# Gated inputs of a two-layer decoder trunk: token scales behind fewer or more gates, low parts on GpSimd, two halves in one PSUM bank

## The chip, the cores and the metric

The program runs on one core of one Trainium2 chip. The metric is device time in microseconds for one execution, the median over the runs of a comparison. All tensors are float32; the kernel splits every operand of a product into a high part, which TensorE takes in its reduced float32 form (`fp32r`), and a low part, the remainder, and adds three products (high by high, high by low, low by high). The engines are TensorE (PE; its weight loads are PEld), VectorE (DVE), ScalarE (ACT), GpSimd (POOL) and SyncE (SP), each with a queue of its own that runs in order.

## The reference

Two layers over 512 tokens of width 1024. The part that the change touches closes each layer:

```python
for i in range(DEPTH):
    h = h + 0.5 * swiglu(rmsnorm(h, nw[0]), ffn_w_in[i, 0], ffn_w_out[i, 0])
    hn = rmsnorm(h, nw[1])
    h = h + (retention if i == 0 else forgetting_attention)(hn, ...)
    h = h + 0.5 * swiglu(rmsnorm(h, nw[2]), ffn_w_in[i, 1], ffn_w_out[i, 1])
    gate = jax.nn.sigmoid(rmsnorm(h, nw[3]) @ ple_w_gate[i])      # 1024 x 1024
    h = h + gate * (p[i] @ ple_w_proj[i])                         # p: 512 x 256
return rmsnorm(h, final_norm_w)
```

`rmsnorm` scales each token by the root of its mean square, and `retention` and `forgetting_attention` are the two token mixers.

## The kernel before

Activations lie transposed: `h` is eight blocks of 128 channels by 512 tokens in SBUF (one tile, `hall`). A product with a 1024-wide weight gives one such block, 24 matmuls of 512 columns (8 blocks of the contraction, 3 products each, line 296 to 298 in `mm3`).

Work on TensorE runs in the order in which the program is written. The other engines' orders come from a scheduler that places each instruction by priority when its buffers can be had. Four FFNs are numbered 0 to 3; FFN 1 ends layer 0's chain before the first gated input, FFN 2 opens layer 1, FFN 3 stands before the second gated input.

Weights come through `Weights`: SyncE loads a chunk of 128 x 1024 into one of four raw tiles (`wraw`), ScalarE casts the high part (line 78), and the engine that `W.low` names subtracts to get the low part (line 79). Chunks go into three `w8` tiles, in the order of a plan, two ahead of the one in use. Where `W.low` is `nc.vector`, the low part is VectorE's, where it is `nc.gpsimd`, GpSimd's. A chunk is called hereafter p0, p1 (projection, four output blocks each) and g0 to g7 (gates); the plan is p0, g0 to g4, p1, g5 to g7, and then FFN 2's chunks.

A normalization is not applied ahead of a product: the product runs on `h` times the gain, and its result is multiplied by the token scales. `n.columns()` sums the squares over channels on TensorE (8 small matmuls, line 310) and computes the scales by a short chain on VectorE and ScalarE (lines 446 to 455); `n.rows()` spreads them over the partitions by 4 transposes (line 443) and a copy (line 437) to a tile `rows`.

A gated input (`ple`) has for each of eight output blocks m: a gate product (`gates`, 24 matmuls), a projected input (`added`, 6 matmuls), and `rest`: VectorE multiplies the gate's bank by `rows` (line 1093), ScalarE takes the sigmoid (1094), VectorE multiplies by the projected bank (1097) and adds to `h` (1098). In layer 0 all 512 tokens go at once (`parts == 1`), and behind each `rest` stands `nxt.block(m)`, which makes the eighth part of FFN 2's input forms (lines 353 to 400: sums and differences of token halves on VectorE, high parts on ScalarE, low parts on VectorE) and adds a square to the norm's sum. FFN 2's first two output blocks (`plain`, line 507) need all eight, the last ones at the end of the first half's products. In layer 1 the tokens go in two halves of 256 (`parts == 2`); `W.emit` first issues the chunks up to p0, g0, g1 with the current `W.low`, and the other seven get tiles that stay until the second half: g2 and g3 in eight tiles of a pool `unit_b`, five in a pool of their own. Behind it come the final norm and the output.

PSUM has eight banks of 128 x 512; the pool hands out whole banks, and a bank is free once its last reader is done. The order of work before: added(0..2), gates 0 and 1 interleaved, gate 2, columns, gate 3, rows, added(3), rests 0 to 3, and then gate m, added(m), rest m for m from 4.

Of the kernel before, what the change touches and what calls it, by code (L numbers as in the profile page):

```python
# [54 lines left out]
class Weights:  # L55
# [103 lines left out]
    def take(self, src):  # L159
        assert self.plan[self.used] is src  # L160
        self.emit(self.used + 1 + LOOKAHEAD)
        self.used += 1
        return self.ready[self.used - 1]
# [9 lines left out]
def trunk(ctx, tc, a):  # L173
    nc = tc.nc
# [15 lines left out]
    W = Weights(nc, wraw, wpool)  # L190

    def unit(pool):
        return pool.tile([P, S], F32R, name="unit_" + {id(ua): "a", id(ub): "b", id(uc): "c", id(ud): "d"}[id(pool)])
# [17 lines left out]
    ple_g = [[a["ple_gate"][l, m] for m in range(KB)] for l in range(2)]  # L211
# [60 lines left out]
    def bank():  # L272
        return psum.tile([P, S], F32, name="bank")

    def temp(dtype=F32):
        return tmp.tile([P, S], dtype, name="tmp")
# [18 lines left out]
    def mm3(out, wh, wl, xh, xl, first, last):  # L295
        nc.tensor.matmul(out, wh, xh, start=first, stop=False)  # L296
        nc.tensor.matmul(out, wh, xl, start=False, stop=False)  # L297
        nc.tensor.matmul(out, wl, xh, start=False, stop=last)  # L298
# [158 lines left out]
    def proj(srcs, n, out=None, cols=slice(0, S), take=W.take):  # L457

        ws = [take(s) for s in srcs]
        os = out or [bank() for _ in ws]  # L460
        for k in range(KB):
            ks = slice(k * P, (k + 1) * P)
            for o, (wh, wl) in zip(os, ws):
                mm3(o, wh[:, ks], wl[:, ks], n.hi[k][:, cols], n.lo[k][:, cols], k == 0, k == KB - 1)
        return os
# [595 lines left out]
    def ple(l, n, nxt, phi, plo, parts=1):  # L1061

        w = S // parts
        with ExitStack() as pools:
            if parts > 1:
                W.emit(W.limit)
                W.pool = pools.enter_context(tc.tile_pool(name="wkept", bufs=KEPT - 2, reuse_waits="tile"))
                W.spare = [lambda: unit(ub)] * 8
                W.limit = len(W.plan)
            ws = {}  # L1070

            def weights(src):
                if id(src) not in ws:
                    ws[id(src)] = W.take(src)
                return ws[id(src)]

            for part in range(parts):
                ts_ = slice(part * w, (part + 1) * w)

                def gates(ms):  # L1080
                    return proj([ple_g[l][m] for m in ms], n, [bank()[:, :w] for _ in ms], ts_, weights)

                def added(m):
                    wp = weights(ple_p[l][m // 4])
                    o = bank()[:, :w]
                    for k in range(2):
                        ks = slice(((m % 4) * 2 + k) * P, ((m % 4) * 2 + k + 1) * P)
                        mm3(o, wp[0][:, ks], wp[1][:, ks], phi[k][:, ts_], plo[k][:, ts_], k == 0, k == 1)
                    return o

                def rest(m, g, o):
                    t1, t2, hm = temp()[:, :w], temp()[:, :w], h[m][:, ts_]
                    nc.vector.tensor_tensor(out=t1, in0=g, in1=n.r[:, ts_], op=ALU.mult)
                    nc.scalar.activation(t1, t1, AF.Sigmoid)
                    if parts > 1 and m == KB - 1:
                        nc.scalar.activation(warm, t1[:, 0:1], AF.Sqrt)
                    nc.vector.tensor_tensor(out=t2, in0=o, in1=t1, op=ALU.mult)
                    nc.vector.tensor_tensor(out=hm, in0=hm, in1=t2, op=ALU.add)
                    if parts == 1:
                        nxt.block(m)  # L1100
                    else:
                        nxt.new = m == 0
                        nxt.square(m, ts_, keep=m == KB - 1)
                        nc.gpsimd.tensor_scalar(out=hm, in0=hm, scalar1=fw[:, m : m + 1], scalar2=None, op0=ALU.mult)

                m = 0
                if part == 0:
                    os = [added(m) for m in range(3)]
                    gs = gates((0, 1))
                    W.low = nc.gpsimd if nxt.forms is None else nc.vector  # L1110
                    gs += gates((2,))
                    n.columns()
                    gs += gates((3,))
                    n.rows()
                    os.append(added(3))
                    for m in range(4):
                        rest(m, gs[m], os[m])
                    m = 4
                while m < KB:
                    g = gates((m,))[0]  # L1120
                    rest(m, g, added(m))
                    if part > 0 and m == 2:
                        diag = final_scale(nxt, slice(ts_.start - w, ts_.start))
                    if part > 0 and m == 4:
                        final(diag, slice(ts_.start - w, ts_.start))
                    m += 1
            W.low = nc.vector
            if parts > 1:
                final(final_scale(nxt, ts_), ts_)

    def final_scale(n, ts_):

        w = ts_.stop - ts_.start
        nb = w // P
        totals = [bank() for _ in range(nb)]
        for i, t in enumerate((n.acc[:, ts_], n.kept)):
            for j in range(nb):
                nc.tensor.matmul(
                    totals[j][:, 0:2], t[:, j * P : (j + 1) * P], ones[:, 0:2], start=i == 0, stop=i == 1
                )  # L1140
        r, v, t = (stat.tile([P, nb], F32, name=x) for x in ("last", "cv2", "ct2"))
        for j in range(nb):
            mean_eps(v[:, j : j + 1], totals[j][:, 0:1])
        rsqrt(r, v, t)
        diag = temp()[:, :w]
        nc.vector.tensor_tensor(
            out=diag.rearrange("p (j t) -> p j t", j=nb), in0=ident.unsqueeze(1).to_broadcast([P, nb, P]),
            in1=r.unsqueeze(2).to_broadcast([P, nb, P]), op=ALU.mult,
        )
        return diag  # L1150

    def final(diag, ts_):
        w = ts_.stop - ts_.start
        rows, copy = bank()[:, :w], temp()[:, :w]
        nc.tensor.matmul(rows, ones, diag, start=True, stop=True)
        nc.scalar.copy(copy, rows)
        ov = a["outT"].rearrange("(b p) t -> p b t", p=P)
        for b in range(KB):
            hb = h[b][:, ts_]
            if b < 2:  # L1160
                nc.gpsimd.tensor_tensor(out=hb, in0=hb, in1=copy, op=ALU.mult)
            else:
                nc.vector.tensor_tensor(out=hb, in0=hb, in1=rows, op=ALU.mult)
        for b0, b1, eng in ((2, 4, nc.sync), (4, 6, nc.scalar), (0, 2, nc.scalar), (6, 8, nc.sync)):
            eng.dma_start(out=ov[:, b0:b1, ts_], in_=hall[:, b0:b1, ts_])
# [24 lines left out]
    def ffn_ple(i, l, n, mid, nxt, stack, apool, parts):  # L1190
        phi, plo = [], []

        def load():
            pv = a["pT"][l].rearrange("(b p) t -> b p t", p=P)
            for b in range(2):
                t1 = temp()
                nc.sync.dma_start(out=t1, in_=pv[b])
                phi.append(unit(uc))
                plo.append(unit(uc))
                split(t1, phi[b], plo[b])  # L1200

        ffn(i, n, mid, stack, apool, load)
        stack = open_ffn(i + 1) if i < 3 else None
        ple(l, mid, nxt, phi, plo, parts)
        return stack
# [101 lines left out]
```

## Time and profile before

| | |
|---|---|
| median of 3 runs | 2255.05 us (2253.7 to 2256.75) |
| profiled execution, its own time | 2254.57 us |
| its span in the trace | 2252.8 us |
| mean granted TensorE clock | 0.983 |
| PE busy | 2158.8 us (96%) |
| DVE busy | 1467.5 us (65%) |
| ACT busy | 1211.5 us (54%) |
| POOL busy | 436.7 us (19%) |

Times in the trace are from the start of the span. The first gated input runs on TensorE from about 1137.6 to 1196.6 us, FFN 2's first output block from there to 1226.7; the second gated input begins at about 2173 us and reaches to the end. A row of a timeline gives the start, the duration, engine, line, operation, tiles, shape and count, and in brackets the idle time of the engine just before and what ended it. Where a wait hangs on several events, the row names the one that came last.

### The profile page before, as it was taken

Reading aid. Unit: us, or ns where it says so; the run is one execution under the profiler, and the core shown is the slowest. Engines: PE = TensorE matmul, PEld = TensorE weight load, DVE = VectorE, ACT = ScalarE, POOL = GpSimd, SP = SyncE. Lnnn points to the kernel's source line nnn. Section 1 sums busy time; section 2 is a strip of 40 time slices with the busy share of each in tenths; the row PEclk is TensorE's granted clock in tenths of the full one; section 3 lists DMA queues with packets and bytes.
Section 4 is the critical chain, followed back from the end, with each engine's and each line's share of the span. In section 5 each row is a group of like instructions: output and inputs, shape, how many; then the busy total and the mean of one; then the engine's idle time right before and its main releaser. Section 6 shows DMA issues by size and latency. Waiting matters only on the chain.

```text
span 2252.8 us, 34423 instructions
## 1 busy us (share of the span) xinstructions
PE 2158.8 (96%) x13501; PEld 1940.0 (86%) x13501; DVE 1467.5 (65%) x2661; ACT 1211.5 (54%) x2050; POOL 436.7 (19%) x326
## 2 busy tenths in 40 slices
PE   7999999999999899999997999999899999999998
PEld 7899997888888698988976999898778798999987
DVE  8686766353442876766758677775764686877764
ACT  7465553333233664554545656464786775554553
POOL 0010003444444010110110001013333200110144
PEclk9999999999999999999998999999999999999999
DMA  5465462222222354654522456463222234655531
GB/s 179 104 164 150 137 159 94 88 90 84 86 84 75 108 144 128 154 137 122 133 97 85 113 150 164 129 166 94 88 81 76 75 105 116 166 146 143 150 103 38
DMA packets 84882, 264.98 MB, mean 118 GB/s; under 512 B 9312, under 2 KB 12896, under 8 KB 84720
## 3 DMA queue, kind: packets, MB, share of 16 engines
q1 hardware_dynamic: 63328, 209.78, 28.2%
q0 software_dynamic: 20160, 51.91, 13.8%
q8 instruction: 106, 1.74, 0.3%
q10 hardware_dynamic: 1232, 1.09, 0.2%
q14 instruction: 56, 0.46, 0.1%
HBM read 260.62 MB, written 2.13 MB: 117 GB/s over the span
## 4 chain that ended last, share of the span: by engine, by line
PE 78%; DVE 8%; ACT 6%; issue 3%; DMA 3%; POOL 1%; SPq 0%; DVEq 0%; ACTq 0%; POOLq 0%
PE bank L476 30%; PE bank L298 13%; PE bank L296 13%; PE bank L297 13%; DMA wraw<-in_ffn_w_in 3%; PE bank L507 2%; PE bank L679 2%; PE bank L680 2%; PE bank L681 2%; DVE w L79 1%; DVE sums L140 1%; ACT p L982 1%; ACT w L78 1%; POOL w L79 1%; ACT p L984 1%
## 5 line engine op out<-in xcount | busy, mean ns | idle before, releaser
L78 ACT CAST w<-wraw 128x1024 fp32r<-128x1024 f32 (+1 forms) x245 | 248.6, 1022 | 456.0 <-PE bank L298 276.0
L298 PE MATMUL bank<-unit_a,w 128*128 128x512 f32 x736 | 287.4, 391 | 4.8 <-DVE w L79 3.1
L296 PE MATMUL bank<-unit_a,w 128*128 128x512 f32 x736 | 288.8, 392 | 2.1 <-ACT w L78 2.1
L78 ACT CAST s<-sums 128x512 fp32r<-128x512 f32 x328 | 197.7, 617 | 166.2 <-DVE sums L140 113.8
L297 PE MATMUL bank<-unit_a,w 128*128 128x512 f32 x736 | 286.9, 390 | 0.2 <-DVE unit_a L288 0.2
L79 DVE TENSOR_TENSOR s<-sums,s 128x512 fp32r<-128x512 f32 x328 | 220.4, 685 | 90.6 <-ACT s L78 90.1
L298 PE MATMUL bank<-unit_d,w 128*128 128x512 f32 (+1 forms) x712 | 270.2, 380 | 6.4 <-DVE w L79 6.4
L296 PE MATMUL bank<-unit_d,w 128*128 128x512 f32 (+1 forms) x712 | 271.2, 381 | 2.8 <-ACT w L78 1.8
L79 POOL TENSOR_TENSOR w<-wraw,w 128x1024 fp32r<-128x1024 f32 x90 | 217.0, 2414 | 287.2 <-ACT w L78 275.3
L297 PE MATMUL bank<-unit_d,w 128*128 128x512 f32 (+1 forms) x712 | 270.2, 379 | 1.8 <-DVE unit_d L288 1.8
L79 DVE TENSOR_TENSOR w<-wraw,w 128x1024 fp32r<-128x1024 f32 (+1 forms) x155 | 179.5, 1164 | 40.2 <-ACT w L78 40.0
L118 POOL DMA_DIRECT2D a<-in_ffn_w_in x82 | 71.8, 876 | 684.9 <-ACT a L117 531.8
L476 PE MATMUL bank<-unit_b,s 128*128 128x256 f32 x904 | 191.3, 278 | 0.0
L476 PE MATMUL bank<-unit_a,s 128*128 128x256 f32 x1314 | 188.4, 281 | 2.0 <-ACT unit_a L360 1.0
L476 PE MATMUL bank<-unit_d,s 128*128 128x256 f32 x1140 | 179.0, 277 | 0.0
L476 PEld LDWEIGHTS bank<-unit_a,s 128*128 128x128 f32 x1314 | 169.8, 192 | 3.0 <-ACT unit_a L360 1.2
L568 DVE SCALAR_TENSOR_TENSOR tmp<-bank,rows 128x512 f32<-128x512 f32 x96 | 66.0, 689 | 162.8 <-PE bank L298 161.5
L298 PEld LDWEIGHTS bank<-unit_a,w 128*128 128x128 f32 x736 | 138.2, 188 | 36.1 <-DVE w L79 5.3
L296 PEld LDWEIGHTS bank<-unit_a,w 128*128 128x128 f32 x736 | 138.3, 188 | 32.8 <-ACT w L78 4.5
L298 PEld LDWEIGHTS bank<-unit_d,w 128*128 128x128 f32 x712 | 136.0, 191 | 32.6 <-DVE w L79 8.3
L297 PEld LDWEIGHTS bank<-unit_a,w 128*128 128x128 f32 x736 | 138.3, 188 | 28.3 <-DVE unit_a L288 0.5
L296 PEld LDWEIGHTS bank<-unit_d,w 128*128 128x128 f32 x712 | 136.3, 191 | 30.2 <-ACT w L78 3.4
(266 smaller groups left out, 4754.4 us busy)
## 6 DMA issues: line engine op xcount, KB each, us to landing
wraw<-in_ffn_w_in SPq DMA_DIRECT2D x174, 512.0 KB, 4.2
wraw<-in_ffn_w_out SPq DMA_DIRECT2D x64, 512.0 KB, 5.1
w<-in_ffn_w_in POOLq DMA_DIRECT2D x58, 512.0 KB, 5.5
a<-in_ffn_w_in POOLq DMA_DIRECT2D x82, 256.0 KB, 6.2
wraw<-in_ffn_w_out SPq DMA_DIRECT2D x32, 384.0 KB, 3.8
wraw<-in_ret_qk SPq DMA_DIRECT2D x16, 512.0 KB, 3.5
wraw<-in_ret_v SPq DMA_DIRECT2D x16, 512.0 KB, 3.6
wraw<-in_ret_g SPq DMA_DIRECT2D x16, 512.0 KB, 3.5
```

The lines of the kernel that those rows point to most:

```text
L78: self.nc.scalar.copy(hi, raw)
L79: self.low.tensor_tensor(out=lo, in0=raw, in1=hi.bitcast(F32), op=ALU.subtract)
L118: self.nc.gpsimd.dma_start(out=lo, in_=src, accum_op=ALU.add)
L296: nc.tensor.matmul(out, wh, xh, start=first, stop=False)
L297: nc.tensor.matmul(out, wh, xl, start=False, stop=False)
L298: nc.tensor.matmul(out, wl, xh, start=False, stop=last)
L476: add = lambda w, x, start, stop: nc.tensor.matmul(out, w, x, start=start, stop=stop, skip_group_check=True)
L507: nc.tensor.matmul(o[:, HALVES[t]], x[:, ks], y, start=k == t == q == 0, stop=k == KB - 1 and q == 2, skip_group_check=True,)
L568: nc.vector.scalar_tensor_tensor(out=t1, in0=o, scalar=-0.5, in1=n.r, op0=ALU.mult, op1=ALU.mult)
L679: nc.tensor.matmul(os[t], xh, wh[:, js], start=k == 0, stop=False)
L680: nc.tensor.matmul(os[t], xh, wl[:, js], start=False, stop=False)
L681: nc.tensor.matmul(os[t], xl, wh[:, js], start=False, stop=k == KB - 1)
```

## The change

Only `ple` is changed.

In layer 0 `W.low` is GpSimd from the start of the gated input to its end (it was VectorE throughout), so g1 to g7, p1 and FFN 2's first two chunks get their low parts there. The order becomes added(0..2), gate 0, columns, gate 1, rows, added(3), rest 0, gate 2, rest 1, gate 3, rests 2 and 3, and on from m = 4 as before: the scales stand behind one gate (columns) and two (rows), where they stood behind three and four.

In layer 1 the two products of an output block share one bank, the projected input in the left 256 columns, the gate in the right. The order becomes added(0..3), gates 0 to 3 interleaved, columns, gate 4, rows, rests 0 to 3, added(4), rest 4, and on from m = 5; the second half of the tokens keeps its order. `W.low` is GpSimd from before the first product (it was set after gates 0 and 1), which moves the low parts of g2 and g3 as well.

```diff
+                both = {}
+                def half(m, i):
+                    if parts == 1:
+                        return bank()
+                    if m not in both:
+                        both[m] = bank()
+                    return both[m][:, i * w : (i + 1) * w]
+
                 def gates(ms):
-                    return proj([ple_g[l][m] for m in ms], n, [bank()[:, :w] for _ in ms], ts_, weights)
+                    return proj([ple_g[l][m] for m in ms], n, [half(m, 1) for m in ms], ts_, weights)
                 def added(m):
                     wp = weights(ple_p[l][m // 4])
-                    o = bank()[:, :w]
+                    o = half(m, 0)
...
                 if part == 0:
-                    os = [added(m) for m in range(3)]
-                    gs = gates((0, 1))
-                    W.low = nc.gpsimd if nxt.forms is None else nc.vector
-                    gs += gates((2,))
+                    W.low = nc.gpsimd
+                    os = [added(m) for m in range(2 + parts)]
+                    gs = gates((0,)) if parts == 1 else gates((0, 1, 2, 3))
                     n.columns()
-                    gs += gates((3,))
+                    m = len(gs)
+                    gs += gates((m,))
                     n.rows()
-                    os.append(added(3))
-                    for m in range(4):
+                    if parts == 1:
+                        os += [added(3)]
+                        rest(0, gs[0], os[0])
+                        gs += gates((2,))
+                        rest(1, gs[1], os[1])
+                        gs += gates((3,))
+                    for m in range(2 if parts == 1 else 0, 4):
                         rest(m, gs[m], os[m])
                     m = 4
+                    if parts > 1:
+                        rest(4, gs[4], added(4))
+                        m = 5
                 while m < KB:
                     g = gates((m,))[0]
                     rest(m, g, added(m))
```

After the change the lines of `rest` are ten further down: 1093, 1094, 1097 and 1098 become 1103, 1104, 1107 and 1108.

How instructions move is seen at three places. First VectorE in the first gated input, from the last step of the token scales (L452) to the first form (L372); the numbered tiles `w` are weight chunks, here p1 and g5 in the numbering of before:

```order
 L452 SCALAR_TENSOR_TENSOR cols<-ct,cols 128x4
-L79 TENSOR_TENSOR w_11130<-wraw,w_11130 128x1024
-L1093 TENSOR_TENSOR tmp<-bank,rows 128x512
-L1097 TENSOR_TENSOR tmp<-bank,tmp 128x512
-L1098 TENSOR_TENSOR hall<-hall,tmp 128x512
-L79 TENSOR_TENSOR w_11263<-wraw,w_11263 128x1024
+L1103 TENSOR_TENSOR tmp<-bank,rows 128x512
+L1107 TENSOR_TENSOR tmp<-bank,tmp 128x512
+L1108 TENSOR_TENSOR hall<-hall,tmp 128x512
 L372 TENSOR_TENSOR tmp<-tmp 128x256
```

The low parts of weights are gone from VectorE's queue; the rest's three instructions and the forms keep their order. One weight low (FFN 2's third chunk, `w_11521`) stays on VectorE, between the last L1103 and the last L1107.

Then ScalarE at the end of the first gated input, after the change; `w_11444` and `w_11521` are FFN 2's second and third chunks, `a` and `s` its first pair:

```order
L78 CAST w_11444<-wraw 128x1024
L365 ACTIVATE tmp<-hall,small 128x512
L290 ACTIVATE unit_a<-hall,small 128x256
L368 CAST unit_d<-tmp 128x256
L360 CAST unit_d<-tmp 128x256
L412 ACTIVATE tmp<-hall 128x512
L78 CAST w_11521<-wraw 128x1024
L1104 ACTIVATE tmp<-tmp 128x512
L116 CAST a_11660<-wraw 128x512
L117 ACTIVATE a_11660<-wraw 128x512
L78 CAST s_11656<-sums 128x512
L380 ACTIVATE tmp<-hall,small 128x512
```

Before, the casts of those two chunks stood next to each other ahead of block 4's forms, where they now stand on either side of block 6's; L380 at the end is the start of block 7's forms.

Last GpSimd before the second gated input, where `acc` is the norm's sum of squares. Before:

```order
L79 TENSOR_TENSOR w_21807<-wraw,w_21807 128x1024
L79 TENSOR_TENSOR w_21855<-wraw,w_21855 128x1024
L416 TENSOR_TENSOR acc<-acc,tmp 128x512
L79 TENSOR_TENSOR w_21938<-wraw,w_21938 128x1024
L79 TENSOR_TENSOR w_21967<-wraw,w_21967 128x1024
L79 TENSOR_TENSOR w_21990<-wraw,w_21990 128x1024
```

Now, from the fourth addition on:

```order
+L416 TENSOR_TENSOR acc<-acc,tmp 128x512 x4
+L79 TENSOR_TENSOR unit_b<-wraw,unit_b 128x512
+L416 TENSOR_TENSOR acc<-acc,tmp 128x512
+L79 TENSOR_TENSOR unit_b<-wraw,unit_b 128x512 x2
+L416 TENSOR_TENSOR acc<-acc,tmp 128x512
+L79 TENSOR_TENSOR unit_b<-wraw,unit_b 128x512
+L79 TENSOR_TENSOR w_21763<-wraw,w_21763 128x1024
+L79 TENSOR_TENSOR w_21768<-wraw,w_21768 128x1024
+L416 TENSOR_TENSOR acc<-acc,tmp 128x512
```

Four halves of g2 and g3 (`unit_b`) have come from VectorE in among the additions, ahead of g4 and p1. In the same listing of waits, L1103 of an output block in the second gated input now waits for TensorE's projected input as well, and L1107 behind it waits for ScalarE alone.

## The prediction

> **What bounds the kernel now.** I read the page first, then the chain of waits, the TensorE timeline with its waits, the table of stretches, and the VectorE, ScalarE and GpSimd timelines at the same places.
>
> ```profile
> span 2252.8 us, 34423 instructions
> PE 78%; DVE 8%; ACT 6%; issue 3%; DMA 3%; POOL 1%; SPq 0%; DVEq 0%; ACTq 0%; POOLq 0%
> ```
>
> TensorE carries the chain, so only stretches where it waits can give time. The TensorE timeline (start, us, engine, line, tiles, and in brackets the idle time before and its releaser) has these in and behind the two gated inputs:
>
> ```profile
> 1141.68 0.39 PE L296 MATMUL bank<-unit_a,w 128*128 128x512 f32 x1
> ...
> 1153.23 0.50 PE L296 MATMUL bank<-unit_a,w 128*128 128x512 f32 x1 [0.50 <-ACT w L78]
> 1154.48 0.50 PE L298 MATMUL bank<-unit_a,w 128*128 128x512 f32 x1 [0.52 <-DVE w L79]
> 1167.82 0.50 PE L296 MATMUL bank<-unit_c,w 128*128 128x512 f32 x1 [1.23 <-ACT rows L437]
> 1196.63 0.75 PE L507 MATMUL bank<-unit_b,w 128*128 128x256 f32 x5
> ...
> 1217.87 2.16 PE L507 MATMUL bank<-unit_c,w 128*128 128x256 f32 x6 [3.32 <-ACT unit_c L360]
> 1226.68 0.95 PE L310 MATMUL bank<-ones_r,tmp 128*128 128x2 f32 x8
> ...
> 2179.78 0.58 PE L298 MATMUL bank<-unit_d,w 128*128 128x256 f32 x1 [3.69 <-DVE w L79]
> 2195.17 0.38 PE L296 MATMUL bank<-unit_c,w 128*128 128x256 f32 x1 [0.68 <-ACT rows L437]
> ```
>
> The table of stretches gives us, busy time (and count) by engine, granted clock, DMA share:
>
> ```profile
> 1137.60:1196.60 59.00, 56.75 (x253) 46.17 (x252) 33.05 (x56) 28.31 (x42) 2.10 (x2) 1.00 0.27 89
> 1196.60:1226.70 30.10, 16.56 (x98) 14.74 (x97) 27.75 (x51) 19.02 (x36) 1.76 (x2) 0.72 0.32 87
> 2179.80:2184.80 5.00, 5.00 (x23) 5.00 (x24) 2.81 (x2) 4.14 (x6) 4.79 (x3) 0.50 0.29 105
> ```
>
> Gated input 0 keeps TensorE busy 56.75 of 59 us. The big hole is behind it: FFN 2's first block, 96 matmuls of 256 columns, takes 30.1 us with VectorE busy for 27.75. The last forms it needs (unit_c, from block 7) come at 1217.8, and the rest after them takes 8.8 (1217.87 to 1226.68). So gated input 0 is worth what it does to VectorE's chain of rests and forms. The first and last of those rests are dated by their last addition to h (VectorE timeline), and the forms by ScalarE's high part:
>
> ```profile
> 1170.57 0.69 DVE L1098 TENSOR_TENSOR hall<-hall,tmp 128x512 f32<-128x512 f32 x1
> 1177.96 0.69 DVE L1098 TENSOR_TENSOR hall<-hall,tmp 128x512 f32<-128x512 f32 x1
> 1185.05 0.69 DVE L1098 TENSOR_TENSOR hall<-hall,tmp 128x512 f32<-128x512 f32 x1
> 1189.46 0.69 DVE L1098 TENSOR_TENSOR hall<-hall,tmp 128x512 f32<-128x512 f32 x1
> 1194.96 0.48 DVE L291 SCALAR_TENSOR_TENSOR unit_a<-hall,small,unit_a 128x256 fp32r<-128x256 f32 x1
> 1196.35 0.68 DVE L1098 TENSOR_TENSOR hall<-hall,tmp 128x512 f32<-128x512 f32 x1
> 1202.43 0.68 DVE L1098 TENSOR_TENSOR hall<-hall,tmp 128x512 f32<-128x512 f32 x1
> 1209.91 0.68 DVE L1098 TENSOR_TENSOR hall<-hall,tmp 128x512 f32<-128x512 f32 x1
> 1214.95 0.68 DVE L1098 TENSOR_TENSOR hall<-hall,tmp 128x512 f32<-128x512 f32 x1
> ...
> 1217.20 0.62 ACT L360 CAST unit_c<-tmp 128x512 fp32r<-128x512 f32 x1
> ```
>
> **Gated input 0: an earlier start.** The three waits before the first rest (0.50, 0.52, 1.23) go, as g2's buffer comes free after one gate and os3 no longer needs the spread's bank. They give nothing by themselves, because FFN 2 then waits for VectorE. The start of the rests counts. A matmul costs 0.23 (56.75 less some 1.5 for columns and spread, over 240), a gate of 24 about 5.5, a projected block of 6 about 1.4. From 1141.7, gate 0 ends at 1147.2, columns at 1148.0, gate 1 at 1153.5, the spread at 1154.1, added(3) at 1155.5. ScalarE then runs, in its new order, a cast, rows, a cast, the table load, the sigmoid, at these durations:
>
> ```profile
> 1166.24 1.04 ACT L78 CAST w<-wraw 128x1024 fp32r<-128x1024 f32 x1 [3.87 <-issue]
> 1167.19 0.58 ACT L437 COPY rows<-bank 128x512 f32<-128x512 f32 x1
> 1167.79 1.28 ACT L1094 ACT_TABLE_LOAD   x1
> 1169.18 0.63 ACT L1094 ACTIVATE tmp<-tmp 128x512 f32<-128x512 f32 x1
> ```
>
> The second cast waits for added(3), so the sigmoid ends at 1158.6, L1107 at 1159.2, and rest 0 at about 1160.1 (it was 1171.3): **11.2 us earlier**. g1's low ahead of the last acc addition costs that sum about 2 us, under gate 0.
>
> **Gated input 0: the lows on GpSimd.** Ten lows move. The groups of L79 (min/median/max ns) price one at 2.39 on GpSimd against 1.22 on VectorE:
>
> ```profile
> L79 POOL TENSOR_TENSOR w<-wraw,w x90: 2345/2394/2875, 370.7 to 2186.7; 128x1024 fp32r<-128x1024 f32 x90
> L79 DVE TENSOR_TENSOR w<-wraw,w x155: 946/1217/1227, 17.9 to 2178.5; 128x1024 fp32r<-128x1024 f32 x123, 128x768 fp32r<-128x768 f32 x32
> ```
>
> They are not off VectorE's path. In gated input 1, where both engines already share the work, the two timelines show:
>
> ```profile
> 2172.72 2.50 POOL L79 TENSOR_TENSOR w<-wraw,w 128x1024 fp32r<-128x1024 f32 x1 [0.34 <-ACT w L78]
> 2175.49 2.55 POOL L79 TENSOR_TENSOR w<-wraw,w 128x1024 fp32r<-128x1024 f32 x1 [0.27 <-ACT w L78]
> ...
> 2173.20 2.57 DVE L79 TENSOR_TENSOR unit_b<-wraw,unit_b 128x512 fp32r<-128x512 f32 x1 [0.27 <-ACT unit_b L78]
> 2175.69 0.68 DVE L568 SCALAR_TENSOR_TENSOR tmp<-bank,rows 128x512 f32<-128x512 f32 x1
> 2176.40 2.19 DVE L571 TENSOR_TENSOR hall<-hall,tmp 128x512 f32<-128x512 f32 x1
> 2178.51 1.21 DVE L79 TENSOR_TENSOR w<-wraw,w 128x1024 fp32r<-128x1024 f32 x1
> ```
>
> A 0.69 us VectorE instruction whose two inputs lie in SBUF ends 0.55 after the GpSimd low that ran when it came (2175.77 against 2175.22, 2178.59 against 2178.04); L568, with a PSUM input, is not held. [...]
>
> L1103 and L1107 read PSUM; L1108 and all form work are exposed. The step from rest 2 to 3 has no low in it: 4.4 us. From 3 to 4 it is 6.9, less two L291 (0.4 each) and a 0.25 rest of a low: 5.85. Seven steps without lows: 4 x 4.4 + 3 x 5.85 = 35.2. Before they took 44.4 (1170.57 to 1214.95), 9.2 for lows, casts waiting for TensorE, L291 and FFN 2's sums. After the change, six lows (p1, g5, g6, g7, FFN 2's first two) fall between rest 0 and rest 7. Stepping both queues by these durations, each low starts as its cast ends, sigmoid and L1107 cover 0.2 to 1.3 of it, and the rest is held: 1.2, 1.8, 2.2, 1.4, 2.2, 2.4, in all 11.2. Four L291 1.6, the one low left on VectorE 1.2, one sum 0.6 (the others come behind rest 7), casts 0.8: 50.6. So rest 7 ends at 1210.7, and L380, one cast and the high part (0.72 + 0.5 + 0.6) put unit_c at 1212.5 instead of 1217.8. TensorE then needs the same 8.8, since it has waited as long: **-5.3 us**. Bounds: nothing held gives unit_c near 1201.3 and, with the clock up, 53 matmuls of 0.12 behind it, so 1207.7 instead of 1226.7: -19. Six times the longest low (2.88) is 17.3: +0.8. I take 11.2 since the rows show the full hold whenever the two meet.
>
> **Gated input 1.** TensorE stops at g1's low (3.69) and then runs 23 matmuls at clock 0.50, 0.21 apart instead of 0.12, 2.1 more. That low is late by a hold (L571 above). Now GpSimd also takes g2 and g3 in four halves (1.2 each) ahead of g4, p1. L568 comes at 2174.2, L571 behind the last half at 2175.9, then g4's low holds g1's until 2178.2, so TensorE goes on at 2179.4: -0.4. added(3) now runs before the wait (6 x 0.12 = -0.7), and the wait for rows goes, since shared banks leave one free (-0.7). The sharing costs at the end: L1103 now waits for added(m) as well, as both lie in one bank. Only the last block has no cover for it:
>
> ```profile
> 2239.13 0.28 PE L296 MATMUL bank<-unit_c,w 128*128 128x256 f32 x1
> 2239.72 0.28 PE L298 MATMUL bank<-unit_c,w 128*128 128x256 f32 x1
> ...
> 2239.40 0.42 DVE L1093 TENSOR_TENSOR tmp<-bank,rows 128x256 f32<-128x256 f32 x1 [1.31 <-PE bank L298]
> ```
>
> The multiply moves behind 2240.0: +0.7. Together **-1.1**. Bounds: g1's low never late, -5.8; two full holds more, +1.3. The wait would be 2.7 us. [...] No row here shows a wait of that length.
>
> **Sum.** 2254.57 (profiled execution, span 2252.8) - 5.3 - 1.1 = 2248.1; the median lies 0.5 higher: **2248.5**.
>
> **Rivals.** (1) Little is held: the lows fall into VectorE's waits for ScalarE. -19 and -1.1 to -5.8 give 2230 to 2235; with half of the 11.2 held it is 2242. For: VectorE idles after each sigmoid. Against: each low starts with its cast, right ahead of L1108. (2) The gain is given back: held time reaches 16.5 instead of 11.2, or gated input 1 loses what remains: 2252 to 2256. For: lows up to 2.88. (3) Slower: FFN 2's next pairs come late. Their sums now stand behind rest 7, and their chunks load into buffers that GpSimd frees later.
>
> ```profile
> 1232.43 0.69 DVE L140 TENSOR_TENSOR sums<-wraw 128x512 f32<-128x512 f32 x1 [1.16 <-DMA wraw<-in_ffn_w_in]
> ```
>
> VectorE already waits for such a load 7.6 us before the second block ends (1240.0). If the loads slip by more than 7.6 against TensorE, two pairs wait, each for its four sums and their four lows (8 x 0.69) and a cast (0.6): 12.3 us, less the 6.4 won, is 2261. My walk has them slip by about 2.
>
> **How the numbers follow.** No change is within 0.2%, 4.5 us, about what a measurement of this kernel can tell: 2250.5 to 2259.6. Forecast 0.52, own range 2244 to 2252.5 (0.42 of it faster); rival 1 0.20; rival 2 0.19; rival 3 0.09 (0.07 of it beyond 2259.6). Faster 0.62, same 0.31, slower 0.07. The range, 2238 to 2257, takes in rival 2 and of rival 1 what keeps a third of the hold.
>
> **What would show it.** Rest 0 ends near 1160; the L1108 rows last 1 to 2.7 us where a GpSimd L79 runs; FFN 2's first block still ends on unit_c, near 1212, and L310 behind it comes near 1221; TensorE waits for g1's low until 2179 less some 5 us; the last L1103 follows added(7). Wrong if L1108 keeps 0.69 (rival 1), if rest 7 is not earlier than 1214 (rival 2), or if FFN 2 waits for sums or loads after its second block (rival 3).

## The result

The changed kernel takes 2241.97 us (median of 4 runs, 2239.65 to 2247.52) against 2255.9 us of the kernel before: ratio 0.9942, 95% interval 0.9921 to 0.9963. Measured once more beside three of the experiments it was 2238.78 us against 2251.87, ratio 0.9949 (0.9932 to 0.9967). It is 11 to 13 us faster; 6.4 had been forecast, 2248.5, with a range of 2238 to 2257.

Where the time went is read by cutting both profiled executions at the same instructions: the first projected product of gated input 0, the first L476 row (FFN 2's third block, behind the two blocks that need the whole gated input), and the first projected product of gated input 1. TensorE timeline, before (start, us, engine, line, tiles, and in brackets the wait ahead with its releaser):

```profile
1137.60 0.39 PE L296 MATMUL bank<-unit_c,w 128*128 128x512 f32 x1
...
1240.04 0.40 PE L476 MATMUL bank<-unit_b,w 128*128 128x256 f32 x2
...
2173.17 0.28 PE L296 MATMUL bank<-unit_c,w 128*128 128x256 f32 x1
```

The same view of the changed kernel, with the waits of over 1 us in the second and the fourth stretch but for the two of the final norm at the end (1.98 and 1.80; before 1.87 and 1.80):

```profile
span 2237.8 us, 34424 instructions
...
1135.08 0.39 PE L296 MATMUL bank<-unit_c,w 128*128 128x512 f32 x1
...
1197.32 0.80 PE L507 MATMUL bank<-unit_b,w 128*128 128x256 f32 x2 [5.71 <-ACT w L78]
1200.52 3.14 PE L507 MATMUL bank<-unit_b,w 128*128 128x256 f32 x13 [2.40 <-POOL w L79]
...
1208.12 0.38 PE L507 MATMUL bank<-unit_c,w 128*128 128x256 f32 x1 [1.50 <-ACT unit_c L360]
...
1217.09 0.95 PE L310 MATMUL bank<-ones_r,tmp 128*128 128x2 f32 x8
...
1230.45 0.64 PE L476 MATMUL bank<-unit_b,w 128*128 128x256 f32 x4
...
2160.65 0.28 PE L296 MATMUL bank<-unit_c,w 128*128 128x256 f32 x1
...
2166.44 0.58 PE L298 MATMUL bank<-unit_d,w 128*128 128x256 f32 x1 [2.16 <-DVE w L79]
```

The 15.0 us between the two spans fall into four parts: up to gated input 0 2.5 (1137.60 against 1135.08), from there to FFN 2's third block 7.1 (102.44 against 95.37), from there to gated input 1 2.9 (933.13 against 930.20), and from there to the end 2.5 (79.63 against 77.15). On TensorE only the second and the fourth hold changed work (two of the half lows that moved run on GpSimd just ahead of the last cut, and TensorE waits for neither). The other 5.4 lie where both kernels run the same instructions: what they are is told with the clock, below. The second execution of the changed kernel has 93.90 and 75.67 in those two stretches, 8.5 and 4.0 less than before.

The table of stretches (us, busy time and count by engine, granted clock, DMA share) for gated input 0, for FFN 2's first block, and behind the wait in gated input 1:

```profile
1135.10:1191.10 56.00, 56.00 (x253) 46.24 (x252) 35.79 (x52) 28.73 (x44) 23.99 (x11) 1.00 0.25 84
1191.10:1217.10 26.00, 15.75 (x98) 14.85 (x97) 22.45 (x39) 16.11 (x30) 4.01 (x2) 0.80 0.32 91
2166.40:2169.60 3.20, 3.16 (x15) 3.16 (x15) 2.81 (x1) 0.52 (x1) 3.20 (x2) 0.50 0.82 279
```

TensorE never waits in gated input 0 now (56.00 of 56.00, before 56.75 of 59), and FFN 2's first block takes 26.0 us instead of 30.1. What dates that block is VectorE's chain of rests and forms. VectorE and then GpSimd timeline of the changed kernel:

```profile
1156.78 0.95 DVE L1108 TENSOR_TENSOR hall<-hall,tmp 128x512 f32<-128x512 f32 x1
1161.85 1.74 DVE L1108 TENSOR_TENSOR hall<-hall,tmp 128x512 f32<-128x512 f32 x1
1167.53 2.29 DVE L361 TENSOR_TENSOR unit_b<-tmp,unit_b 128x512 fp32r<-128x512 f32 x1
1174.87 2.80 DVE L1108 TENSOR_TENSOR hall<-hall,tmp 128x512 f32<-128x512 f32 x1
1183.38 1.75 DVE L1108 TENSOR_TENSOR hall<-hall,tmp 128x512 f32<-128x512 f32 x1
1188.85 2.80 DVE L1108 TENSOR_TENSOR hall<-hall,tmp 128x512 f32<-128x512 f32 x1
...
1198.18 2.57 DVE L291 SCALAR_TENSOR_TENSOR unit_a<-hall,small,unit_a 128x256 fp32r<-128x256 f32 x1
...
1205.61 0.68 DVE L1108 TENSOR_TENSOR hall<-hall,tmp 128x512 f32<-128x512 f32 x1
```

```profile
1160.64 2.40 POOL L79 TENSOR_TENSOR w<-wraw,w 128x1024 fp32r<-128x1024 f32 x1 [3.46 <-ACT w L78]
1166.86 2.41 POOL L79 TENSOR_TENSOR w<-wraw,w 128x1024 fp32r<-128x1024 f32 x1 [3.82 <-ACT w L78]
1174.73 2.39 POOL L79 TENSOR_TENSOR w<-wraw,w 128x1024 fp32r<-128x1024 f32 x1 [5.46 <-ACT w L78]
1182.17 2.40 POOL L79 TENSOR_TENSOR w<-wraw,w 128x1024 fp32r<-128x1024 f32 x1 [5.06 <-ACT w L78]
1188.70 2.40 POOL L79 TENSOR_TENSOR w<-wraw,w 128x1024 fp32r<-128x1024 f32 x1 [4.13 <-ACT w L78]
1197.34 3.12 POOL L79 TENSOR_TENSOR w<-wraw,w 128x1024 fp32r<-128x1024 f32 x1 [6.24 <-ACT w L78]
```

Each of these six lows on GpSimd has a VectorE row of two SBUF inputs beside it that ends 0.55 behind it (1177.67 against 1177.12; the last one 0.29) and lasts up to 2.80 instead of 0.69. Beyond the rows' own durations (0.69, and 0.47 for L291) VectorE stands still for 1.05, 1.60, 2.11, 1.06, 2.11 and 2.10 us, and 0.26 in the first row, behind an earlier low: 10.3 in all. Rest 0 ends 22.65 us after the start of the input, rest 7 71.21. TensorE comes late to FFN 2's first block as well: it waits 5.71 and 2.40 us for the block's weights, and then only 1.50 for the last forms (0.36 to 1.50 in the five executions with this input 0). By these rows a chain that ended earlier by more than that would have had to wait for TensorE.

### The profile page after: what moved, and what is told of

It reads as the page before. It is cut to its first block, busy times and chain, and to the rows that moved or that the text cites. A ratio compares the mean times of both kernels' runs of the same rounds, so it can differ in the third digit from the quotient of the medians.

```text
span 2237.8 us, 34424 instructions
## 1 busy us (share of the span) xinstructions
PE 2149.4 (96%) x13501; PEld 1931.8 (86%) x13501; DVE 1466.9 (66%) x2647; ACT 1210.3 (54%) x2050; POOL 470.4 (21%) x340
## 4 chain that ended last, share of the span: by engine, by line
PE 78%; DVE 8%; ACT 7%; issue 3%; DMA 3%; POOL 1%; SPq 0%; DVEq 0%; ACTq 0%; POOLq 0%
PE bank L476 31%; PE bank L298 13%; PE bank L296 13%; PE bank L297 13%; DMA wraw<-in_ffn_w_in 2%; PE bank L507 2%; PE bank L679 2%; PE bank L680 2%; PE bank L681 2%; ACT p L982 1%; DVE w L79 1%; ACT p L984 1%; DVE sums L140 1%; ACT w L78 1%; DVE tlo L288 1%
## 5 line engine op out<-in xcount | busy, mean ns | idle before, releaser
L79 POOL TENSOR_TENSOR w<-wraw,w 128x1024 fp32r<-128x1024 f32 x100 | 243.2, 2435 | 323.4 <-ACT w L78 304.7
L476 PE MATMUL bank<-unit_b,s 128*128 128x256 f32 x904 | 190.5, 277 | 0.0
L476 PE MATMUL bank<-unit_a,s 128*128 128x256 f32 x1314 | 188.5, 281 | 1.9 <-ACT unit_a L360 1.0
L79 DVE TENSOR_TENSOR w<-wraw,w 128x1024 fp32r<-128x1024 f32 (+1 forms) x145 | 169.6, 1175 | 20.8 <-ACT w L78 20.7
L476 PE MATMUL bank<-unit_d,s 128*128 128x256 f32 x1140 | 178.4, 276 | 0.0
L476 PEld LDWEIGHTS bank<-unit_a,s 128*128 128x128 f32 x1314 | 169.7, 192 | 2.9 <-ACT unit_a L360 1.2
L568 DVE SCALAR_TENSOR_TENSOR tmp<-bank,rows 128x512 f32<-128x512 f32 x96 | 66.0, 689 | 161.5 <-PE bank L298 159.1
L118 POOL DMA_DIRECT2D w<-in_ffn_w_in x58 | 50.7, 874 | 550.9 <-ACT w L117 468.0
L298 PEld LDWEIGHTS bank<-unit_d,w 128*128 128x128 f32 x712 | 134.3, 189 | 30.8 <-DVE w L79 6.8
```

Of the source, the lines that this page charges most:

```text
L79: self.low.tensor_tensor(out=lo, in0=raw, in1=hi.bitcast(F32), op=ALU.subtract)
L118: self.nc.gpsimd.dma_start(out=lo, in_=src, accum_op=ALU.add)
L476: add = lambda w, x, start, stop: nc.tensor.matmul(out, w, x, start=start, stop=stop, skip_group_check=True)
L568: nc.vector.scalar_tensor_tensor(out=t1, in0=o, scalar=-0.5, in1=n.r, op0=ALU.mult, op1=ALU.mult)
```

## Experiments

All are read by the same three cuts. "Input 0" is the time from the first projected product of gated input 0 to FFN 2's third block, "forms" the time from that start to the first matmul of FFN 2 on `unit_c` (the last forms), "between" the time from the third block to gated input 1, "input 1" from there to the end. The ratio is to the kernel before, on the same chip, with its 95% interval.

| kernel | input 0 | forms | between | input 1 | ratio |
|---|---|---|---|---|---|
| before | 102.44 | 80.27 | 933.13 | 79.63 | 1 |
| changed | 95.37 | 73.04 | 930.20 | 77.15 | 0.9942 (0.9921 to 0.9963) |
| changed, again | 93.90 | 73.05 | 930.22 | 75.67 | 0.9949 (0.9932 to 0.9967) |
| input 0: new order, lows on VectorE; input 1 as before | 95.06 | 69.63 | 939.30 | 79.86 | 0.9984 (0.9972 to 0.9996) |
| input 0: old order, lows on GpSimd; input 1 as before | 105.41 | 82.09 | 936.92 | 79.94 | 1.0015 (1.0003 to 1.0028) |
| input 0 as before; input 1 as changed | 103.34 | 80.23 | 932.41 | 77.18 | 0.9988 (0.9975 to 1.0002) |
| changed, lows among the rests on VectorE | 93.07 | 69.65 | 937.39 | 77.18 | 0.9958 (0.9943 to 0.9973) |
| changed, two banks for the last block | 93.88 | 73.04 | 932.71 | 76.09 | 0.9943 (0.9927 to 0.9959) |
| changed, g4's and p1's lows of input 1 on VectorE | 93.90 | 73.06 | 931.63 | 76.85 | 0.9947 (0.9931 to 0.9964) |
| the last three edits together | 92.91 | 69.67 | 937.74 | 74.84 | 0.9954 (0.9937 to 0.9970) |
| changed, lows among the rests by transfer | 103.01 | 82.57 | 932.54 | 77.21 | 0.9987 (0.9975 to 0.9999) |
| changed, g2's and g3's lows of input 1 on VectorE | 93.93 | 73.09 | 934.45 | 78.06 | 0.9951 (0.9935 to 0.9966) |

**The order of input 0 alone.** In the changed program, for `parts == 1`:

```diff
-                    W.low = nc.gpsimd
+                    W.low = nc.vector
```

and the old code, order and banks, for `parts == 2`.

> Gated input 0 in its new order, but with the low parts of its weights on VectorE as before; gated input 1 wholly as before. Theory (an earlier start of the rests is what gives; a low costs VectorE about as much as standing still behind GpSimd's low, 1.22 against 10.3 over seven): TensorE's first L507 wait ends on unit_c some 7 to 10 us earlier than before, so 2246 to 2249 against 2255.9 of before. Rival (the gain is VectorE being rid of the lows): the rests start early but each waits for a low behind a late cast, as before; 2 to 4 us faster, 2252 to 2254.

VectorE's rows of the first and last addition to h, and TensorE's wait for the last forms:

```profile
1157.37 0.69 DVE L1108 TENSOR_TENSOR hall<-hall,tmp 128x512 f32<-128x512 f32 x1
...
1203.16 0.68 DVE L1108 TENSOR_TENSOR hall<-hall,tmp 128x512 f32<-128x512 f32 x1
```

```profile
1205.31 0.58 PE L507 MATMUL bank<-unit_c,w 128*128 128x256 f32 x1 [2.54 <-ACT unit_c L360]
```

The last forms come 10.6 us earlier than before (69.63 against 80.27), a little more than the theory said, and 3.4 earlier than in the changed kernel: the seven rests behind the first take 45.8 us (1157.37 to 1203.16, two rows of equal length) instead of 48.6 (from the end of the row at 1156.78 to that of the row at 1205.61). Before, they took 44.4, so they gain nothing in themselves. Input 0 as a whole gains 7.4. So in this stretch the order gives the gain, and the lows on GpSimd make the chain longer. The time, 0.16% or 3.6 us faster (0.04 to 0.28%), is less than the 7.4 of the stretch, and by itself would fit the rival's 2 to 4; against the rival stands the date of the forms alone. This run's profiled execution has 939.30 in the stretch between, with the instructions of before in the same order, 6.2 more than there: 3.9 of it are longer waits of TensorE, and one window of 3.41 us more at half clock makes up to 1.7.

**The lows of input 0 alone.**

```diff
+                    W.low = nc.gpsimd if parts == 1 else W.low
                     os = [added(m) for m in range(3)]
```

and `W.low` stays GpSimd behind gates 0 and 1.

> Only the lows of gated input 0 go to GpSimd, its order of work and gated input 1 stay as before. Theory: no earlier start, g2's low 1.2 later, held time of VectorE (10) in place of its own lows (7 to 9): between -1 and +2 us, 2255 to 2258. Rival (lows off VectorE are the gain): 5 us faster, 2251.

```profile
1154.38 0.50 PE L298 MATMUL bank<-unit_a,w 128*128 128x512 f32 x1 [1.70 <-POOL w L79]
```

Slower by 0.15%, and by 3.0 in the stretch: there is no earlier start. TensorE waits longer for the later low of g2 (1.70 instead of 0.52), rest 0 ends 1.1 later (34.74 against 33.66 from the start of the input), the seven rests behind it take 45.5 instead of 44.4, and another 1.15 of the 3.0 come behind the last forms. The rival, by which VectorE being rid of the lows is the gain, falls.

**Input 1 alone.** The changed code for `parts == 2`, the old one for `parts == 1`.

> Gated input 1 as changed, gated input 0 as before. Theory: the wait for g1's low shrinks from 3.69 to about 2.2, ten fewer matmuls at half clock, no wait for rows, 0.7 given back at the last block: 2.6 us faster, 2253.3. Rival (the two inputs' shares are the other way round, the rest of the measured 13 us lies here): 6 us or more faster, 2250 or below.

2.5 us less in the stretch (77.18 against 79.63), 0.12% in the time, whose interval ends at 1.0002. That is the theory's 2.6; the rival, by which 6 us or more lie here, falls. Taken alone, the two inputs make 3.6 and 2.7 us, 6.3 together, where the whole change makes 11 to 13. The stretches do add up (7.4 and 2.5 against 7.1 to 8.5 and 2.5 to 4.0), so the difference lies outside them; the intervals reach 3 to 5 us to either side, and no run here settles it.

**VectorE not held among the rests.** In input 0:

```diff
                         gs += gates((2,))
+                        W.low = nc.vector
                         rest(1, gs[1], os[1])
```

> The changed kernel, with only the lows of g1 to g4 on GpSimd in gated input 0 (while VectorE has little to do) and p1, g5 to g7 and FFN 2's first two on VectorE, among the rests. Theory (a held VectorE instruction costs what it is held): 10 us of holding goes, six lows of 1.22 come, 2.7 us faster than the changed kernel's 2242: 2239. Rival (a low in VectorE's queue makes the rests behind it wait for its cast): 2242 to 2247.

The held time goes as expected: no L1108 row behind the first lasts longer than 0.69, and the last forms come 3.4 us earlier (69.65 against 73.05). But input 0 gains only 0.8 of it against the second execution of the changed kernel, and the time doesn't show it. TensorE timeline of this kernel, and of the changed one's second execution:

```profile
1203.21 0.58 PE L507 MATMUL bank<-unit_d,w 128*128 128x256 f32 x1 [3.14 <-ACT unit_d L368]
...
1208.21 0.58 PE L507 MATMUL bank<-unit_c,w 128*128 128x256 f32 x1 [2.54 <-ACT unit_c L360]
...
1217.07 0.95 PE L310 MATMUL bank<-ones_r,tmp 128*128 128x2 f32 x8
1220.61 1.58 PE L507 MATMUL bank<-unit_b,w 128*128 128x256 f32 x11 [1.89 <-DVE w L79]
```

```profile
1208.96 0.38 PE L507 MATMUL bank<-unit_c,w 128*128 128x256 f32 x1 [1.32 <-ACT unit_c L360]
...
1216.44 0.95 PE L310 MATMUL bank<-ones_r,tmp 128*128 128x2 f32 x8
1218.79 1.46 PE L507 MATMUL bank<-unit_b,w 128*128 128x256 f32 x10 [0.69 <-DVE w L79]
```

From the last forms to L310 it is 8.86 us here and 7.48 there, and the next weight low is waited for 1.89 instead of 0.69, since it stands behind two sums in VectorE's queue. The tables of stretches for those two pieces:

```profile
1208.20:1217.10 8.90, 8.74 (x55) 8.45 (x56) 6.69 (x13) 4.48 (x9) 0.87 (x1) 0.74 0.18 60
```

```profile
1209.00:1216.40 7.40, 6.76 (x54) 6.56 (x55) 6.17 (x11) 3.17 (x7) 0.00 (x0) 1.00 0.31 77
```

With the lows on VectorE, TensorE's waits stand right ahead of the last forms (3.14 and 2.54) and the work behind them runs at clock 0.74; with the lows on GpSimd the long waits (5.71, 2.40) come earlier, at FFN 2's first weights, and here the clock is full again (1.00) by the last forms. So 1.4 us go to the clock and 1.2 to the low. The theory's 2.7 us did not come; the time, 0.9958, is some 2246 of the 2255.9, where the rival put it, though not for the rival's reason: the seven rests take 45.6 us here against 48.6.

**Two banks for the last block.**

```diff
-                    if parts == 1:
-                        return bank()
+                    if parts == 1 or part > 0 and m == KB - 1:
+                        return bank()[:, :w]
```

> The changed kernel, with two banks again for the last output block of the second half, so that its L1103 needn't wait for the projected input. Theory (sharing costs 0.7 at the end): gated input 1 from its start to the end takes 76.4 instead of 77.15 us, L1103 starts under the last projected input. Rival (the end hangs on GpSimd or the norm's last sum): 77.1 as before. In the whole time 0.7 is below what can be told.

VectorE timeline at the last L1103, changed kernel and then this one:

```profile
2224.36 0.42 DVE L1103 TENSOR_TENSOR tmp<-bank,rows 128x256 f32<-128x256 f32 x1 [1.25 <-PE bank L298]
```

```profile
2222.16 0.42 DVE L1103 TENSOR_TENSOR tmp<-bank,rows 128x256 f32<-128x256 f32 x1 [0.55 <-PE bank L298]
```

0.70 us less, as the sharing was priced, and 1.06 in the stretch (76.09 against 77.15, both with half clock behind the wait for g1's low: matmuls 0.21 us apart); the other 0.36 is not traced. The rival falls: TensorE waits about 0.3 us for GpSimd's last sum in both kernels, and 1.29 instead of 1.98 for the norm's last square. The time can't tell 0.7.

**g4's and p1's lows off GpSimd.** In input 1, ahead of the interleaved gates:

```diff
+                    if parts > 1:
+                        for src in ple_g[l][0:2]:
+                            weights(src)
+                        W.low = nc.vector
                     gs = gates((0,)) if parts == 1 else gates((0, 1, 2, 3))
+                    W.low = nc.gpsimd
```

> The changed kernel, with the lows of g4 and p1 of gated input 1 on VectorE instead of GpSimd, so that no low on GpSimd runs while g1's low is due. Theory (g1's low is late because VectorE is held): its row takes 1.2 instead of 3.4 us, TensorE's wait of 2.16 falls to 0.3 or less, and the half clock behind it goes: the input takes 73.5 to 74.3 instead of 77.15 us, and the kernel is 3 us faster than the changed one. Rival (g1's low is late since its cast or its buffer is, or VectorE has too much to do with two lows more): the wait stays at 1.5 us or grows.

VectorE's row of g1's low in the changed kernel, and its rows at that place in this one:

```profile
2162.97 3.42 DVE L79 TENSOR_TENSOR w<-wraw,w 128x1024 fp32r<-128x1024 f32 x1
```

```profile
2162.23 2.24 DVE L79 TENSOR_TENSOR w<-wraw,w 128x1024 fp32r<-128x1024 f32 x1 [1.25 <-ACT w L78]
2164.40 0.68 DVE L568 SCALAR_TENSOR_TENSOR tmp<-bank,rows 128x512 f32<-128x512 f32 x1
2165.11 0.69 DVE L571 TENSOR_TENSOR hall<-hall,tmp 128x512 f32<-128x512 f32 x1
2165.72 2.35 DVE L79 TENSOR_TENSOR w<-wraw,w 128x1024 fp32r<-128x1024 f32 x2
```

g1's low (the first of the two at 2165.72) is no longer held, yet TensorE still waits 1.81 instead of 2.18: the scheduler put g4's low ahead of L568, where it waits for its cast (1.25), is itself held by the last half of g3 (2.24), and pushes L568, L571 and g1's low back. That lows on GpSimd hold g1's low is shown (3.42 us in the changed kernel against 1.2 here); that taking them away ends the wait is not, since the edit put another low in the way. The rival was right about the time.

**All three.** 

> All three edits in one: only g1 to g4's lows on GpSimd in gated input 0, g4's and p1's on VectorE in gated input 1, two banks for its last block. Theory: 2.3 + 3.2 + 0.7 = 6 us faster than the changed kernel, 16 faster than before, 0.993. Rival (what gated input 0 wins is given back in FFN 2, whose sums and loads then come late): 0.995 or more.

92.91 and 74.84, the least of all kernels in both stretches, by 1.0 and 0.8 against the changed kernel's second execution; the time is 0.9954, no faster than the changed kernel. The 3 to 4 us by which such gains would show are smaller than the spread of the stretch between (937.74 here, 930.20 to 939.30 over all). That doesn't rule out the rival, by which FFN 2 gives the gain back: the three kernels with lows on VectorE among the rests in the new order have the three longest stretches between (937.39 to 939.30; the others 930.20 to 936.92). The instructions and their order are the same there in all of them, and one trace of each can't tell a cause from chance.

**The changed kernel again.** 

> The changed kernel itself once more, beside the next three. Read stage by stage in the traces, the change gave 7.1 us between the start of gated input 0 and FFN 2's second block, and 2.5 between the start of gated input 1 and the end. Theory (the rest of the 14.9 between the two profiled executions lies in stretches whose instructions are the same, at half clock more often in one than in the other): 9.6 us faster than before, 0.9957. Rival (all of it belongs to the change): 0.9942 or less again.

0.9949, with 93.90 and 75.67 in the two stretches: 8.5 and 4.0 faster than before, 12.5 in all, against 11.5 by the ratio. The interval, 0.9932 to 0.9967, holds the theory's 0.9957 and the rival's 0.9942, so the time decides nothing between them. The two stretches themselves differ by 1.5 each from one execution to the next, which the theory's 9.6 had left out.

**The lows by transfer.** In input 0, where `W.low` was set to VectorE above, p1, g5 to g7 and FFN 2's first two get the FFN chunks' way of making a low part (lines move by three to four):

```diff
-        self.split(raw[:, :n], t[:, 0, :n], t[:, 1, :n])
+        if self.low is None:
+            self.negated(raw[:, :n], t[:, 0, :n], t[:, 1, :n], src)
+        else:
+            self.split(raw[:, :n], t[:, 0, :n], t[:, 1, :n])
```

> The changed kernel, with the six lows that are made among the rests of gated input 0 (p1, g5 to g7, FFN 2's first two) made by ScalarE (minus the high part) and an accumulating transfer, as the FFNs' own chunks are, so that neither VectorE nor GpSimd computes them. Theory (VectorE's standing still behind GpSimd's lows is a term of its chain): no L1108 or form row over 0.7; from the end of rest 0 to the end of rest 7 38.5 to 42 us instead of 48.6, FFN 2's last forms 62 to 67 us behind the start of the input instead of 73.05, and FFN 2's third block at 87 to 91 instead of 93.9. Rival (the lows come too late this way, since such a transfer lands 5.5 us after its issue): TensorE waits inside gated input 0, and FFN 2's third block starts at 94 or later.

```profile
1176.49 0.79 PE L301 MATMUL bank<-unit_a,w 128*128 128x512 f32 x1 [5.19 <-DMA w<-in_ple_gate]
```

The rows of issues of this kernel, between 1160 and 1180 us, have such a transfer at

```profile
w<-in_ple_gate POOLq DMA_DIRECT2D x2, 512.0 KB, 8.2
```

8.2 us from issue to landing, not 5.5. The rival was right: a gate's low part comes too late, TensorE stands still for 5.19 us inside the input, later for 2.50 more, and for 7.69 in FFN 2's first block, each time for such a transfer, and everything behind follows (103.01). Whether a chain with no low on either engine would have run as fast as the theory says is left open by this.

**g2's and g3's lows of input 1 back on VectorE.**

```diff
-                    W.low = nc.gpsimd
+                    W.low = nc.gpsimd if parts == 1 else nc.vector
                     os = [added(m) for m in range(2 + parts)]
+                    if parts > 1:
+                        for src in ple_g[l][0:2]:
+                            weights(src)
+                        W.low = nc.gpsimd
```

> The changed kernel, with only the lows of g2 and g3 in gated input 1 back on VectorE; order and shared banks as changed. Theory (these four halves are what shortens the wait for g1's low): TensorE waits 3.2 to 3.7 again instead of 2.17, with two stretches at half clock; the input takes 78.5 to 79.5 us. Rival (the order and the banks give the 2.5 us): wait about 2.2, 77.2 or less.

```profile
2171.86 0.58 PE L298 MATMUL bank<-unit_d,w 128*128 128x256 f32 x1 [3.08 <-DVE w L79]
```

Between the two, and 0.4 short of the theory's 78.5: the wait is 3.08 (3.69 before, 2.16 changed), the stretch 78.06 (79.63 and 77.15). g1's low comes 6.72 us behind the start of the input here, 6.61 before and 5.79 in the changed kernel, so the four halves are what dates it, by 0.9 us; that the wait is yet 0.6 shorter than before is added(3), which now runs ahead of it. Order and banks give the other 1.6 of the 2.5, some 0.8 of it by the clock: about 14 matmuls 0.21 us apart behind the wait, where before there were 23.

## Why the prediction was right, and where its sizes were off

**The bound and the start of the rests.** Right: FFN 2's first block waited for VectorE's chain and still does, and the three waits removed lie ahead of longer waits for that chain, so that by the traces they gave nothing by themselves (no run takes them away alone). Rest 0 was to end 22.5 us after the start of the input (1160.1 less 1137.60) and ends at 22.65. The experiment with the order alone shows that this start is the gain.

**The held time.** Right in kind, nearly right in size: 11.2 us were forecast over six lows, 10.0 are there, 10.3 with the first row. What the price was weighed against is now measured: six lows on VectorE make the seven rests 45.8 us long, six on GpSimd 48.6. The longest hold among the rests makes a 0.69 us addition last 2.80 us, beside a low of 2.40 on GpSimd. For VectorE's chain this part of the change was a loss, as the run with the lows alone shows (the seven rests 45.5 us instead of 44.4, the time 0.15% slower). In the time of the whole kernel it can't be told: with these lows back on VectorE it is 0.9958, against 0.9942 and 0.9949.

**The last forms.** Forecast 74.9 us after the start (1212.5 less 1137.6), measured 73.04: 1.9 too late. All of it lies between rest 0 and rest 7, which take 48.6 instead of the 50.6 of the sum: 1.2 of that is held time, and some 0.8 is in the other terms, which I did not trace one by one.

**The 8.8 us behind them.** This step failed: "TensorE then needs the same 8.8, since it has waited as long". It needs 8.97 us in one execution of the changed kernel and 7.48 in the other (and in the three experiments that keep its input 0), for TensorE did not wait as long for the forms (1.50 and 1.32 us instead of 3.32): its long waits are now the 5.71 and 2.40 for FFN 2's weights, further ahead, which the prediction did not have, and the clock is mostly full again by the last forms (0.81 over the piece in the first execution and 1.00 in the second, 0.75 before). Where the piece takes 8.97, 3.41 us of it (1210.58 to 1213.99) are at half clock. That is 1.3 us more gain in most executions.

**Gated input 1.** Mis-sized term: the wait for g1's low was to be 2.7 (the prediction's own terms, 3.69 less 0.4 and 0.7, give 2.6) and is 2.16, and no gain was booked for the clock behind it, where 23 matmuls at half speed became 14 in one execution and none in the other (0.8 to 2.1 us). The wait for rows went, as forecast, and the tail cost its 0.7. So 2.5 to 4.0 instead of 1.1. The clock behind the wait came out both ways: behind 2.16 the table of stretches shows 0.50; in the other execution, behind 2.18, it stayed full, and the input takes 75.67 us instead of 77.15. By the record of the clock, 2.03 us of the first wait lie within one of the windows described below, while the second is split over two, 0.49 and 1.69.

**The sum.** 5.3 became 7.1 to 8.5, 1.1 became 2.5 to 4.0; the sum of 6.4 (which makes 2248.2, not 2248.1) was about half of what was measured, and the range held it since its lower end was drawn for a case with little held. That case is not what happened, as VectorE was held for 10 us, so that the range held the time was in part luck. Of the 3.2 to 6.1 us by which the two stretches gained more than forecast, the forms make 1.9, the wait for g1's low 0.5, and the clock 0.6 to 3.4, by execution. Rival 3 was wrong: FFN 2's second block waits for a low (0.69, as before), not for sums or loads. Nor did rival 2 come, though the GpSimd lows did cost what it feared, 3.4 us at the last forms.

## What to carry to other kernels

Price the start of a chain that a stage waits for, not the waits in front of it: here 2.25 us of TensorE's waits lay ahead of longer ones and by the traces were worth nothing in themselves, and the 11 us by which VectorE's chain could start earlier were worth 7 to 8 in that stretch. A low moved from VectorE to GpSimd was not off VectorE here: VectorE's rows with two SBUF inputs beside such a low lasted up to 2.80 us instead of 0.69, so that a low of 1.2 us was traded for up to 2.1 us of standing still. And where TensorE waited mattered beside how long: behind the same wait of 1.8 us the same work took 43.30 us in one execution and 44.97 in another, by where the wait fell, as the next section shows.

## What the hardware showed that I had not expected

A stretch with the same instructions differs between executions by one step of about 1.7 us. From the wait at FFN 2's third block to the next wait of its chunks, in the changed kernel's second execution and in the one with the lows among the rests on VectorE:

```profile
1240.55 0.51 PE L476 MATMUL bank<-unit_b,w 128*128 128x256 f32 x2 [1.78 <-ACT tmp L528]
...
1283.85 0.51 PE L296 MATMUL bank<-unit_a,w 128*128 128x512 f32 x1 [0.29 <-ACT w L78]
```

```profile
1242.37 0.50 PE L476 MATMUL bank<-unit_b,w 128*128 128x256 f32 x2 [1.77 <-ACT tmp L528]
...
1287.34 0.50 PE L296 MATMUL bank<-unit_a,w 128*128 128x512 f32 x1 [0.29 <-ACT w L78]
```

43.30 and 44.97 us behind the same wait of 1.8. Each trace records the granted clock. In each of the twelve, all its changes from the first to the last lie on one grid of 3.413 us, to within 2 ns. The tables of stretches for the grid's window in which the wait ends, and for the next one, in the same two executions (TensorE is busy for 2.00 of the 3.41 us in the first and for 1.64 in the second):

```profile
1239.14:1242.55 3.41, 2.00 (x17) 2.00 (x17) 2.99 (x8) 2.32 (x6) 0.00 (x0) 1.00 0.31 108
1242.55:1245.96 3.41, 3.41 (x33) 3.41 (x32) 1.64 (x4) 3.35 (x6) 0.88 (x1) 1.00 0.00 0
```

```profile
1240.09:1243.50 3.41, 1.64 (x14) 1.44 (x13) 3.41 (x8) 2.37 (x5) 0.00 (x0) 1.00 0.53 160
1243.50:1246.92 3.42, 3.42 (x18) 3.42 (x17) 0.97 (x2) 2.62 (x3) 0.00 (x0) 0.50 0.02 5
```

In the twelve executions this piece is 43.3 us eight times and 45.0 to 45.1 four times. In those four the wait ends 0.60 to 1.13 us before its window does, so that all of it lies in one window, and the next window runs at half clock. In the eight it ends 0.52 us or less before the window's end or is split over two windows. So in these twelve, where the wait falls on the grid tells the two cases apart.

A step of 1.7 us is one window of 3.41 us at clock 0.50, and the wait in the window ahead of it fills about half of that one, 1.77 us of 3.41.

The same records give most of the 5.4 us outside the changed stretches. Up to gated input 0 and between, 44.4 us run at half clock before and 27.3 in the changed kernel. These are five windows fewer, worth up to 8.5 us, while TensorE's waits there are 1.6 us longer. The second execution of the changed kernel has 30.7 us at half clock in the same places, and one kernel's runs spread over more (2245.69 to 2255.89 for before, in 12 runs) than the edits of 1 to 3 us that were compared.
